# A two-layer hybrid decoder step on one core: sample state updates moved into the feed-forward stage, with four smaller changes of order

## The chip, the cores and the metric

The kernel runs on one core of one Trainium2 chip. The metric is the device time of one execution in microseconds (us); where several runs are given, the median is used, and the spread stands beside it.

## What is computed

The reference is one inference step of two layers. A layer normalises x, projects it, runs three mixers side by side on parts of the projection, multiplies their joined outputs with `w_out`, and adds; then a gated feed-forward network (FFN) with a causal convolution of width 3 follows. At the end there is one more norm. Cut to what matters here:

```python
h = rmsnorm(x);  proj = h @ w_in
rq, rk, rv, rg, su, gq, gk, gv, gg, glr = split(proj)
o_ret, s_ret_new = retention_chunked(rotary(rq), rotary(rk), rv, s_ret)   # 6 heads of 64
o_ret = groupnorm(o_ret) * silu(rg)
o_s5 = gelu(s5_scan(su));  o_s5 = o_s5 * sigmoid(o_s5 @ glu_w + glu_b)
o_gla, s_gla_new = gla_chunked(gq, gk, gv, log_sigmoid(glr @ gate_w + gate_b) / 16, s_gla)   # 4 heads
o_gla = rms(o_gla) * silu(gg)
x = x + concat([o_ret, o_s5, o_gla]) @ w_out
a, gate = split(rmsnorm(x) @ ffn_w_in)
x = x + (gelu(conv3(a)) * gate) @ ffn_w_out
y = rmsnorm(x)                                                            # after both layers
```

Two groups of tokens share the weights: a prompt of 512 tokens that starts from a zero state, and eight samples of 4 new tokens each (32 columns) that start from given states. Besides y, the new state of each mixer is an output. For a sample, the output of a head needs the old state; the new state (old state, decayed, plus keys times values) is needed by nothing else in the step. That is true of retention and of gated linear attention (GLA) alike.

## The kernel before

Activations lie with features on the 128 partitions and the 544 tokens as columns: `x` is eight tiles of 128x544. A product with a weight goes through `product()`: weights and activations are split into a high and a low part, and three passes over two halves of 272 columns make six matmuls of 128x272 for each 128 rows of the weight (a k-tile). A product with eight k-tiles has 48 such matmuls. `weights()` runs ahead of them: for each half unit (four k-tiles, 128x512) a DMA on SyncE's queue (`raw`, three in advance), a cast on ScalarE (`ws<-raw`, the high part), a subtraction on VectorE (`ws<-raw,ws`, the low part); four such `ws` tiles are held. In the trace the matmuls of weight products read `mm<-a,ws`; the small matmuls of the mixers write tiles called `m`. The accumulators `mm` have two buffers in PSUM, the small ones `m` have four. The SBUF pool `c` has ten buffers.

A layer has three stages. `in_proj` makes 24 tiles of 128 columns in the order of `IN_TILES`; `evac` takes each out of PSUM and, for most, multiplies it by `r`, the reciprocal norm that is computed beside the first product. Between these products the streams of the mixers run: GLA and retention in chunk pairs (0,1), (2,3) and the sample chunk (`gla_sample`, `ret_sample`), each followed by a norm (`gla_norm1`, `ret_norm1`) and a tail that transposes the result back; S5 in `s5_fetch` (tables) and `s5_stream` (u is written to DRAM as `ud` and read back as `w<-ud`, then scans and a gated output). `out_proj` makes eight tiles in two parts of four k-tiles; `MIX_TILES` says in which order the eight mixer tiles are used (0 to 2 retention, 3 and 4 S5, 5 to 7 GLA). `ffn` makes 22 pairs of up and gate tiles, with the down products in groups, and in layer 2 its last group is `end()`: the final norm is done for two column halves, `scaled()` prepares x and `output(h)` writes half h.

The order on every engine is made by a planner, `Order`. Each stream is a generator that yields between pieces; it has a priority (`PRI`), the main stream with the weight products has the last one. A piece is issued when its due time on TensorE's planned clock has come and, for priorities with a limit in `LIMITS`, when the engines are planned to be idle enough. `spawn(prio, gen)` starts a stream, `fire(name)` sets an event, `yield name` waits for one. A result is a fixed order of instructions on each engine; the waits between engines are semaphores. All instructions are issued in one helper, so that the trace gives L166 for all of them (L165 in the changed kernel), and they are told apart by their tiles.

At the end of `gla_sample`, after its outputs, stands the update of the sample's state:

```python
ks, vs = stacked(st["kt"], GH * 64, 2), stacked(m.gv[4], GH * GV, 1)   # ACT CAST d<-d, DVE d<-d,d
kt2 = pair_keys(ks, GH)                                                # ACT c<-d,const
vm = pair_values(vs, hd * GV, 2 * GV)                                  # ACT c<-d,const
pe.matmul(kv, lhsT=kt2[...], rhs=vm[...], start=True, stop=True)       # PE m<-c,c
add(ve, sv, sv, kv);  mul(ve, sv, sv, es[...])                         # DVE c<-c,m and c<-c,es
```

`ret_sample` ends in the same way, with a decay by a constant on ScalarE (`c<-c` 128x256) in the place of `c<-c,es`. Each then writes the state out by DMA. The states `S_` of these updates are the tiles that were loaded for the outputs, 2 of 384 KB for GLA and 3 of 256 KB for retention in each layer.

## Time and profile before

| | |
|---|---|
| median of 3 runs | 1382.23 us (1379.76 to 1383.33) |
| the profiled execution, its own time | 1385.73 us |
| its span, first to last instruction | 1383.9 us |
| mean granted TensorE clock | 0.981 of full speed |
| TensorE busy | 1341.8 us, 97% of the span |
| VectorE, ScalarE, GpSimd busy | 881.7, 603.4, 136.2 us |
| DMA | 133.64 MB, 97 GB/s |

The page is one execution, taken by the hardware profiler. A busy time of TensorE is not TensorE at its peak: the granted clock says at which of its two levels (1.2 and 2.4 GHz) it ran. In rows of a timeline, "[1.88 <-DVE c]" means that the engine was idle for 1.88 us before this group and that an instruction of VectorE on a tile c ended the wait; "x66" is the number of instructions in the group. PE is TensorE, PEld its weight loads, DVE VectorE, ACT ScalarE, POOL GpSimd, SP SyncE.

### The profile page before, as it was taken

How to read it: one execution, taken by the hardware profiler on the slowest of the kernel's cores; microseconds unless marked ns; L12 is line 12 of the kernel's file. 1: busy time of each engine (PE TensorE's matmuls, PEld its weight loads, DVE VectorE, ACT ScalarE, POOL GpSimd, SP SyncE). 2: the span in 40 equal slices, each digit the busy share in tenths (PEclk: the TensorE clock that was granted, in tenths of full speed). 3: DMA queues.
4: the chain of work that ended last, by engine and by line, in shares of the span. 5: the costliest groups of instructions: out<-in, count | busy, mean ns of one | idle time of the engine just before them, and what ended most of it. 6: DMA issues, size and time to landing. Idle time of an engine off the chain costs nothing.

```text
span 1383.9 us, 27885 instructions
## 1 busy us (share of the span) xinstructions
PE 1341.8 (97%) x11016; PEld 1314.1 (95%) x11016; DVE 881.7 (64%) x1773; ACT 603.4 (44%) x1256; POOL 136.2 (10%) x358
## 2 busy tenths in 40 slices
PE   6998998999999999999999999999999999999996
PEld 5997997999999999999998999999999999999996
DVE  7876787675567776555667475778655365455456
ACT  4556744553333443333444676346333233233232
POOL 0060000001100460100000000000111011011001
PEclk9999998899999999999998999999999999999998
DMA  5412332232223244323254322123222322322231
GB/s 184 132 51 71 105 98 86 70 94 88 92 80 104 93 131 127 131 67 109 73 169 141 102 80 93 54 91 117 84 84 77 100 92 74 96 92 81 89 98 65
DMA packets 88979, 133.64 MB, mean 97 GB/s; under 512 B 22352, under 2 KB 35088, under 8 KB 88848
## 3 DMA queue, kind: packets, MB, share of 16 engines
q1 hardware_dynamic: 88848, 131.86, 30.6%
q8 instruction: 87, 1.43, 0.4%
q14 instruction: 44, 0.36, 0.1%
HBM read 118.03 MB, written 12.61 MB: 94 GB/s over the span
## 4 chain that ended last, share of the span: by engine, by line
PE 90%; DVE 3%; ACT 2%; POOL 2%; DMA 1%; issue 1%; SPq 1%; DVEq 0%; ACTq 0%; POOLq 0%
PE mm L166 81%; PE m L166 9%; ACT c L166 1%; DVE c L166 1%; POOL a L166 1%; SPq L166 1%; DVE a L166 1%; ACT a L166 0%; DMA x<-in_x 0%; DMA w<-ud 0%; POOL c L166 0%; DVE ws L166 0%; POOL rtq L166 0%; POOL rot L166 0%; ACT ws L166 0%
## 5 line engine op out<-in xcount | busy, mean ns | idle before, releaser
L166 PE MATMUL mm<-a,ws 128*128 128x272 f32 x9408 | 1217.9, 290 | 13.2 <-ACT a L166 8.7
L166 PEld LDWEIGHTS mm<-a,ws 128*128 128x128 f32 x9408 | 1198.0, 190 | 20.1 <-ACT a L166 8.9
L166 ACT CAST ws<-raw 128x512 fp32r<-128x512 f32 (+2 forms) x424 | 249.2, 589 | 485.5 <-PE mm L166 369.2
L166 DVE TENSOR_TENSOR ws<-raw,ws 128x512 fp32r<-128x512 f32 (+2 forms) x424 | 274.5, 652 | 154.0 <-ACT ws L166 153.0
L166 DVE TENSOR_TENSOR c<-mm,r 128x544 f32<-128x544 f32 (+2 forms) x134 | 68.1, 535 | 132.9 <-PE mm L166 128.6
L166 DVE TENSOR_TENSOR x<-x,mm 128x544 f32<-128x544 f32 (+1 forms) x100 | 69.7, 697 | 40.3 <-PE mm L166 38.1
L166 DVE SCALAR_TENSOR_TENSOR w<-c,vec,w 128x560 f32<-128x560 f32 x88 | 71.5, 813 | 16.4 <-ACT w L166 14.6
L166 POOL COPY c<-c 128x2 f32<-128x2 f32 x88 | 34.5, 422 | 435.6 <-DVE c L166 435.6
L166 ACT CAST a<-c 128x544 fp32r<-128x544 f32 x44 | 28.6, 650 | 62.6 <-DVE c L166 52.9
L166 DVE TENSOR_TENSOR a<-c,a 128x544 fp32r<-128x544 f32 x44 | 32.2, 732 | 35.1 <-ACT a L166 35.1
L166 ACT COPY c<-mm 32x544 f32<-32x544 f32 (+1 forms) x60 | 36.4, 607 | 38.9 <-DVE a L166 27.1
L166 POOL MEMSET c<- 128x2 f32 (+4 forms) x54 | 8.6, 160 | 434.2 <-ACT c L166 106.1
L166 POOL TENSOR_TENSOR c<-c,w 128x32 f32<-128x32 f32 x44 | 25.9, 588 | 212.5 <-DVE c L166 175.2
L166 ACT ACTIVATE w<-c,vec 128x560 f32<-128x560 f32 x44 | 37.8, 860 | 8.5 <-DVE c L166 8.5
L166 DVE TENSOR_TENSOR c<-c,w 128x512 f32<-128x512 f32 x44 | 32.4, 737 | 0.0
L166 ACT ACTIVATE c<-c 128x256 f32<-128x256 f32 (+1 forms) x22 | 9.6, 463 | 49.6 <-DVE c L166 49.6
L166 ACT ACTIVATE a<-m,vec 128x128 f32<-128x128 f32 (+2 forms) x68 | 22.6, 413 | 19.1 <-PE m L166 18.9
L166 ACT ACTIVATE w<-w 128x560 f32<-128x560 f32 x44 | 29.6, 672 | 1.7 <-DVE w L166 1.7
L166 ACT ACTIVATE c<-x 128x544 f32<-128x544 f32 (+1 forms) x45 | 24.4, 567 | 7.1 <-DVE x L166 6.7
L166 DVE SCALAR_TENSOR_TENSOR a<-x,vec,a 128x544 fp32r<-128x544 f32 x32 | 24.8, 785 | 4.1 <-ACT a L166 3.3
L166 ACT ACTIVATE a<-x,vec 128x544 fp32r<-128x544 f32 x32 | 23.8, 753 | 7.1 <-DVE x L166 2.8
L166 ACT COPY c<-m 16x128 f32<-16x128 f32 (+3 forms) x51 | 16.6, 326 | 17.1 <-PE m L166 16.7
(187 smaller groups left out, 876.4 us busy)
## 6 DMA issues: line engine op xcount, KB each, us to landing
raw<-in_w_up SPq DMA_DIRECT2D x176, 256.0 KB, 2.8
raw<-in_w_in SPq DMA_DIRECT2D x96, 256.0 KB, 3.0
raw<-in_w_dn SPq DMA_DIRECT2D x64, 256.0 KB, 2.7
raw<-in_w_out SPq DMA_DIRECT2D x32, 256.0 KB, 3.0
raw<-in_w_dn SPq DMA_DIRECT2D x40, 128.0 KB, 2.3
x<-in_x SPq DMA_DIRECT2D x8, 272.0 KB, 5.9
out_y<-a SPq DMA_DIRECT2D x7, 272.0 KB, 2.2
c<-in_sgla SPq DMA_DIRECT2D x4, 384.0 KB, 5.1
```

The lines of the kernel that those rows point to most:

```text
L166: res = f(*args, **kw)
```

## The change

1. The updates of the sample states leave `gla_sample` and `ret_sample` and become streams of their own, `gla_update` and `ret_update`, with priority `late=6` (limit 0.0). They wait for the event `q{l}`, the norm between mixers and FFN, and load the states a second time: ten more DMAs in the two layers, 3 MB.
2. In layer 0, the first three products (su0, su1, gq0) are copied from PSUM to SBUF by ScalarE (`early`), before `r` is known; `evac` then reads the copy. Before, only su0 had a stream of its own, and it was read from PSUM.
3. `MIX_TILES` puts GLA's tiles first in `out_proj`, and S5's tile 4 into the second part.
4. The second table load of S5 (`kpxt`, in `s5_fetch`) waits for the event `U`, which is fired once the load of `w<-ud` is issued, in the place of `us`, which is fired when `ud` is written.
5. In `output`, half 0 is multiplied on VectorE, which takes `r` from PSUM and the gain in the same instruction (before: GpSimd, with a copy of `r`, after VectorE had scaled x by the gain). Of half 1's eight tiles three go to GpSimd (`POOL_OUT`), with a copy of `r` and a scaling of x by ScalarE; its output is written in six pieces, before five.

An unused filler of matmuls in the planner goes as well; it had no instruction in the program but one memset of its operand.

```diff
-MIX_TILES = [3, 4, 5, 6, 7, 0, 1, 2]
+MIX_TILES = [5, 6, 7, 3, 4, 0, 1, 2]
...
-OUT_KS = [[(0, 1), (2, 3), (4, 5), (6, 7)], [(0,), (1, 2), (3, 4), (5, 6), (7,)]]
+EARLY = 3
+
+OUT_KS = [[(0, 1), (2, 3), (4, 5), (6, 7)], [(0,), (5,), (1, 2), (6,), (3, 4), (7,)]]
+
+POOL_OUT = 3
...
-           rotor=3, rotor1=7, fetch=1, out=3)
+           rotor=3, rotor1=7, fetch=1, out=3, late=6)
...
-            r = SM([128, NT], "r", bufs=1) if self.h is None else None if self.h else M3([128, n])
+            r = SM([128, NT], "r", bufs=1) if self.h is None else None
...
-                yield f"us@{l}"
+                yield f"U@{l}"
...
         sy.dma_start(out=U, in_=m.ud.rearrange("s h g n -> (s h) g n"))
         yield
+        fire(m.n("U"))
...
         spawn(PRI["gt"], gla_tail(m, (4,), [st]))
+        spawn(PRI["late"], gla_update(m, st, es))
+
+    def gla_update(m, st, es):
+
+        l = m.l
+        yield f"q{l}"
+        S_ = [M3([128, 2, 4, GV]) for _ in range(2)]
+        for i in range(2):
+            sy.dma_start(out=S_[i].rearrange("p h q c -> p (h q c)"), in_=sgla_in[l, :, i * 8 * GV:(i + 1) * 8 * GV])
+        yield
         ks, vs = stacked(st["kt"], GH * 64, 2), stacked(m.gv[4], GH * GV, 1)
...
         spawn(PRI["rt"], ret_tail(m, (4,), [st]))
+        spawn(PRI["late"], ret_update(m, st))
+
+    def ret_update(m, st):
+        l = m.l
+        yield f"q{l}"
+        S_ = [M3([128, 2, 4, 64]) for _ in range(3)]
+        for i in range(3):
+            sy.dma_start(out=S_[i].rearrange("p h q c -> p (h q c)"), in_=sret_in[l, :, i * 512:(i + 1) * 512])
+        yield
         ks, vs = stacked(st["kt"][0:32].rearrange("p i c -> p (i c)"), RH * 64, 2), stacked(m.rv[4], RH * 64, 1)
...
-            if l == 0 and name == IN_TILES[0]:
-                spawn(0, evac(m, name, pre, i, ps))
+            if l == 0 and name in IN_TILES[:EARLY]:
+                spawn(0, early(m, name, pre, i, ps))
             else:
                 yield from evac(m, name, pre, i, ps)
+
+    def early(m, name, pre, i, ps):
+
+        t = M3([128, NT])
+        se.copy(t, ps)
+        yield
+        yield from evac(m, name, pre, i, t)
...
             yield from nrm[h].feed(x[j][:, cs])
-            if not h:
-                ts(ve, x[j][:, cs], x[j][:, cs], gf(j), None, ALU.mult)
+            if h and j >= 8 - POOL_OUT:
+                se.activation(out=x[j][:, cs], in_=x[j][:, cs], func=AF.Identity, scale=gf(j))
...
             r = rs_[f"r{L}.{h}"]
+            if h:
+                r_ = M3([128, HB])
+                se.copy(r_, r)
             for ks in OUT_KS[h]:
                 t = A([128, 4, HB])
                 for i, k in enumerate(ks):
-                    if not h:
-                        mul(po, t[:, i], x[k][:, cs], r)
+                    if h and k >= 8 - POOL_OUT:
+                        mul(po, t[:, i], x[k][:, cs], r_)
                     else:
                         stt(t[:, i], x[k][:, cs], gf(k), r, ALU.mult, ALU.mult)
+                if not h:
+                    yield 0
```

Because the planner makes the order, these edits move more than their own lines. Three places follow. A name's number is that of its allocation; `x6` at the end of a row is a run of equal rows.

The first place is TensorE at the end of layer 0's `in_proj` and the start of `out_proj`. `mm<-a,ws` are weight products, `m<-Sret`, `m<-d,c` and `m<-d,d` a retention chunk pair's output, `m<-a,c` S5's gate, `m<-c,c` state updates, `m<-a,a` the scores of the next chunk, `m<-const,...` transposes. Before, with the pieces between the shown ones left out:

```order
L166 MATMUL mm_2840<-a_148,ws_2740 128x272 x6
L166 MATMUL m_2911<-Sret,a_1243 128x128 x2
...
L166 MATMUL m_2911<-d_2019,c_2723 128x64 x6
L166 MATMUL m_2921<-d_2019,d_2738 64x64 x6
L166 MATMUL m_2941<-a_2699,c_2703 128x272
...
L166 MATMUL m_2952<-c_2712,c_2289 128x384
L166 MATMUL m_2956<-c_2712,c_2289 128x384
L166 MATMUL m_2963<-a_1243,a_1456 128x128
...
L166 MATMUL m_2983<-Sret,a_1243 128x128 x2
...
L166 MATMUL m_3010<-a_2699,c_2703 128x272
L166 MATMUL mm_2908<-a_2981,ws_2805 128x272 x6
L166 MATMUL m_3045<-a_1243,a_1456 32x32
```

After the change:

```order
L165 MATMUL m_2813<-const,a_1608 128x128 x2
L165 MATMUL mm_2781<-a_142,ws_2633 128x272 x6
L165 MATMUL m_2830<-a_2650,c_2654 128x272
...
L165 MATMUL m_2844<-Sret,a_1207 128x128 x2
L165 MATMUL m_2844<-Sret,a_1442 128x128
L165 MATMUL m_2844<-d_2031,c_2802 128x64 x6
L165 MATMUL m_2854<-d_2031,d_2817 64x64 x6
L165 MATMUL mm_2781<-a_143,ws_2670 128x272 x6
...
L165 MATMUL mm_2781<-a_146,ws_2670 128x272 x6
L165 MATMUL m_2900<-a_1207,a_1442 32x32
...
L165 MATMUL m_2914<-const,a_1608 32x128 x2
L165 MATMUL mm_2923<-a_139,ws_2724 128x272 x6
```

Before, 26 rows of mixer work stand in one block behind the last product of `in_proj`, and one k-tile of `out_proj` (`mm_2908<-a_2981`) stands between that block and the next. Now the same work begins earlier, in shorter pieces, with six to 24 matmuls of weight products between them; the state updates (`m<-c,c`) are gone from here.

The second place is VectorE in layer 0 at the norm of GLA's chunks 0 and 1 (`gv`). Here `c<-D,c` is a scan of S5 (a timeline calls it TENSOR_TENSOR_SCAN), `w<-w,w` a table of S5, `c<-c,a` both a rotary and a part of S5's scan. Before:

```order
L166 TENSOR_TENSOR ws_1257<-raw_1005,ws_1257 128x512
L166 SCALAR_TENSOR_TENSOR c_1297<-D_115_882,c_1203 128x256 x2
L166 TENSOR_TENSOR c_1245<-c_1245,a_720 128x544
L166 TENSOR_TENSOR w_1144<-w_1144,w_1235 128x1152
L166 TENSOR_TENSOR ws_1313<-raw_1086,ws_1313 128x512
L166 TENSOR_TENSOR c_1325<-c_1297,a_881 128x256
L166 TENSOR_TENSOR c_1326<-c_1297,a_881 128x256 x2
L166 TENSOR_TENSOR c_1325<-c_1297,a_881 128x256
L166 TENSOR_REDUCE gv_190_1334<-c_1160 128x4
L166 TENSOR_REDUCE gv_190_1334<-c_1291 128x4
```

After:

```order
L165 TENSOR_TENSOR s5so_595<-s5so_595,m_1282 128x32
L165 TENSOR_TENSOR c_1209<-c_1209,a_695 128x544
L165 TENSOR_TENSOR ws_1270<-raw_1060,ws_1270 128x512
L165 TENSOR_REDUCE gv_188_1316<-c_1146 128x4
L165 TENSOR_REDUCE gv_188_1316<-c_1267 128x4
L165 TENSOR_SCALAR gv_1319<-gv_188_1316 128x8
...
L165 SCALAR_TENSOR_TENSOR c_1437<-D_124_938,c_1280 128x256 x2
L165 TENSOR_TENSOR a_1207<-a_1207,c_1209 128x544
...
L165 TENSOR_TENSOR c_1471<-c_1437,a_937 128x256
L165 TENSOR_TENSOR c_1472<-c_1437,a_937 128x256 x2
...
L165 TENSOR_TENSOR w_1178<-w_1178,w_1247 128x1152
```

Before, the scan, the table sum, one more low part of a weight and four products `c<-c,a` stand ahead of the two reductions; now the reductions follow S5's small sums, one `c<-c,a` and one low part, and the rest comes behind the norm.

The third place is VectorE at the state updates of retention and GLA in layer 0. Before, inside `out_proj`'s first products (`x_89<-x_89,mm_2908` is the first sum of x, `rv` and `mu` belong to the retention norm of the sample chunk):

```order
L166 TENSOR_REDUCE mu_3136<-m_3104 128x6
L166 SCALAR_TENSOR_TENSOR c_3135<-mu_3136,m_3104 128x384
L166 TENSOR_TENSOR d_3140<-d_3063,d_3140 32x384
L166 TENSOR_TENSOR d_3144<-d_2021,d_3144 32x384
L166 TENSOR_TENSOR x_89<-x_89,mm_2908 128x544
L166 TENSOR_REDUCE rv_462_3176<-c_3135 128x6
```

After, in the FFN (`c<-mm,r` is the evacuation of an up product, `w<-c,vec,w` the convolution):

```order
L165 TENSOR_TENSOR c_3670<-mm_3673,r_3755 128x512
L165 TENSOR_TENSOR c_3670<-mm_3673,r_3755 128x8x4
L165 TENSOR_TENSOR ws_3767<-raw_3646,ws_3767 128x512
L165 TENSOR_TENSOR d_3807<-d_1760,d_3807 32x256
L165 TENSOR_TENSOR d_3811<-d_826,d_3811 32x384
L165 SCALAR_TENSOR_TENSOR w_3773<-c_3670,vec,w_3773 128x560 x2
...
L165 TENSOR_TENSOR ws_3984<-raw_3874,ws_3984 128x512
L165 TENSOR_TENSOR c_3790<-c_3790,m_3968 128x384
L165 TENSOR_TENSOR c_3790<-c_3790,es_256_1800 128x384
L165 TENSOR_TENSOR ws_4016<-raw_3916,ws_4016 128x512
```

The splits `d<-d,d` stood between the mean and the variance of the sample's retention norm, ahead of the first sum of x; now they stand between the first products of the FFN, with the updates `c<-c,m` and `c<-c,es` some products later.

## Rows read from the trace of the kernel before

**Rows 1.** The page, part 1: engine, busy time, share of span, instructions.
```profile
PE 1341.8 (97%) x11016; PEld 1314.1 (95%) x11016; DVE 881.7 (64%) x1773; ACT 603.4 (44%) x1256; POOL 136.2 (10%) x358
```

**Rows 2.** Windows: stretch, length, busy PE, PEld, DVE, ACT, POOL; clock, DMA share, GB/s.
```profile
218.00:262.00 44.00, 36.98 (x275) 31.77 (x274) 27.87 (x73) 18.39 (x45) 1.41 (x2) 0.81 0.18 55
300.00:345.00 45.00, 45.00 (x363) 45.00 (x362) 27.06 (x50) 17.64 (x30) 5.01 (x16) 1.00 0.26 83
715.00:740.00 25.00, 22.88 (x156) 20.47 (x156) 12.39 (x29) 7.87 (x13) 0.00 (x0) 0.80 0.59 186
```

**Rows 3.** Chain that ended last: start us, us, engine, tile, instructions.
```profile
307.68 171.09 PE mm L166 x1362
```

**Rows 4.** Timeline, PE, layer 0: start us, us, what [idle before <-releaser].
```profile
220.93 2.10 PE L166 MATMUL m<-a,c 128*128 128x272 f32 x8
...
232.00 3.39 PE L166 MATMUL m<-a,c 128*128 128x272 f32 x8
...
238.76 0.99 PE L166 MATMUL m<-const,c 128*128 128x128 f32 x6 [1.88 <-DVE c L166]
...
242.21 0.44 PE L166 MATMUL m<-c,c 128*32 128x64 f32 x8 [1.66 <-ACT c L166]
...
247.51 10.42 PE L166 MATMUL mm<-a,ws 128*128 128x272 f32 x66
```

**Rows 5.** Timeline of PE, layer 0, start.
```profile
33.06 8.52 PE L166 MATMUL mm<-a,ws 128*128 128x272 f32 x66 [0.90 <-DVE w L166]
...
107.33 1.08 PE L166 MATMUL m<-const,c 128*128 128x128 f32 x6 [1.78 <-DVE c L166]
110.91 6.68 PE L166 MATMUL mm<-a,ws 128*128 128x272 f32 x36 [2.51 <-ACT c L166]
```

**Rows 6.** Timeline of DVE, layer 0, 98 to 109 us.
```profile
98.85 1.27 DVE L166 TENSOR_TENSOR_SCAN c<-D,c 128x256 f32<-128x256 f32 x2
...
103.86 1.01 DVE L166 TENSOR_REDUCE gv<-c 128x4 f32<-128x384 f32 x2
```

**Rows 7.** Timeline of PE and DVE, layer 1.
```profile
728.27 1.24 PE L166 MATMUL m<-w,a 128*64 128x72 f32 x32 [2.12 <-DMA w<-ud]
...
923.82 4.80 PE L166 MATMUL mm<-a,ws 128*128 128x272 f32 x24
929.22 3.25 PE L166 MATMUL mm<-a,ws 128*128 128x272 f32 x24 [0.60 <-DVE x L166]
...
926.09 0.55 DVE L166 TENSOR_TENSOR d<-d,d 32x384 fp32r<-32x384 f32 x1 [0.99 <-ACT d L166]
```

**Rows 8.** Groups by line, ACT and DVE, whole span: busy, mean ns, idle before.
```profile
L166 ACT ACTIVATE c<-d,const 96x128 fp32r<-96x128 f32 (+3 forms) x48 | 17.3, 436 | 0.0
...
L166 ACT CAST d<-d 32x384 fp32r<-32x384 f32 (+1 forms) x16 | 7.7, 483 | 0.3
...
L166 DVE TENSOR_TENSOR c<-c,m 128x384 f32<-128x384 f32 (+1 forms) x14 | 8.5, 606 | 4.8 <-PE m L166 4.8
...
L166 DVE TENSOR_TENSOR c<-c,es 128x384 f32<-128x384 f32 x8 | 4.5, 558 | 0.3
...
L166 DVE TENSOR_TENSOR d<-d,d 32x384 fp32r<-32x384 f32 (+1 forms) x8 | 4.1, 516 | 9.5 <-ACT d L166 9.5
```

**Rows 9.** The same view of ACT, different shapes kept apart.
```profile
L166 ACT COPY c<-mm 128x544 f32<-128x544 f32 x12 | 7.3, 612 | 11.3 <-PE mm L166 11.3
...
L166 ACT ACTIVATE c<-c 128x256 f32<-128x256 f32 x12 | 4.3, 411 | 0.5 <-DVE c L166 0.5
```

**Rows 10.** Timeline of POOL and DVE, end, 1368 to 1381 us.
```profile
1368.76 6.18 POOL L166 TENSOR_TENSOR a<-x,c 128x272 f32<-128x272 f32 x8 [24.17 <-ACT c L166]
...
1370.66 0.42 DVE L166 TENSOR_TENSOR x<-x,mm 128x272 f32<-128x272 f32 x1
...
1372.93 0.60 DVE L166 TENSOR_TENSOR nt<-ny 128x3 f32<-128x3 f32 x1
...
1377.30 3.36 DVE L166 SCALAR_TENSOR_TENSOR a<-x,vec,m 128x272 f32<-128x272 f32 x8 [1.56 <-PE m L166]
```

More of the change, by code (lines that the diff above doesn't have):

```diff
@@ L59 @@
 MARGIN = 25.0
-WARM = 0
-FILLER = ("filler",)
-FILL, FILL_MARGIN = 230.0, 150.0
 V_NMG, V_NFG, V_RNG, V_RNB, V_D, V_GLUB, V_GB, V_GG = 0, 8, 16, 19, 22, 24, 26, 28
@@ L110, in __init__ @@
         self.events = {}
-        self.filler = None
         self.streams = []
@@ L137, in used @@
         self.uses[key] = self.uses.get(key, 0) + 1
-        if self.plan and key[0] != FILLER and self.uses[key] == self.plan["uses"].get(key):
+        if self.plan and self.uses[key] == self.plan["uses"].get(key):
             self.back(name)
@@ L229, in fire @@
         self.events[name] = self.mark
-    def fill(self, now):
-        then = self.free["pe"]
-        n = int((then - now - FILL_MARGIN) / FILL)
-        if n > 0 and len(self.pools.get("m", [0] * 4)) > 1:
-            self.sid = FILLER
-            self.free["pe"] = now
-            self.filler(n)
-            self.free["pe"] = max(then, self.free["pe"])
     def spawn(self, prio, gen):
@@ L257, in run @@
                 self.free["pe"] = min(max(whens[id(s)], now + busy - LIMITS[s[0]]) for s in can)
-                if self.filler and self.free["pe"] < INF:
-                    self.fill(now)
                 assert self.free["pe"] < INF, [(s[4], self.plan["takes"].get((s[4], self.step.get(s[4], 0)))) for s in can]
@@ L354, in trunk @@
     half = cp.tile([128, 1], F32, name="halfc")
-    warm = cp.tile([128, 1, 128], BF16, name="warm")
     trim = cp.tile([128, 2, 128], U8, name="trim")
@@ L1693, in trunk @@
     with tc.manual_schedule():
-        po.memset(warm, 1.0)
         sy.dma_start(out=vec, in_=vec_in)
@@ L1720, in masks @@
             yield
-        def filler(n):
-            ps = MX()
-            for _ in range(n):
-                pe.matmul(ps, lhsT=warm[:, 0], rhs=warm.to_broadcast([128, 4, 128]), start=True, stop=True)
-            order.back(ps.name)
-        order.filler = None
-        order.sid = FILLER
-        filler(WARM)
-        order.sid = ()
         order.free["pe"] = 0.0
```

## Prediction

> **What bounds the kernel now.** I read the page first: TensorE is busy for 1341.8 of 1383.9 us [rows 1]. Some 42 us of idle time are all that a better order can remove directly, and much of that is the start and the end. The chain of waits says the same: its longest piece is 171 us of nothing but weight matmuls, 1362 of them [rows 3]. That piece also gives the price of a matmul at full clock, 171.09 / 1362 = 0.1256 us, so a k-tile (six) costs 0.754 us and a product of eight k-tiles 6.03 us. Then I took windows. In the FFN TensorE is busy for the whole of 300 to 345 us at clock 1.00, while VectorE and ScalarE have 18 and 27 us free of 45 [rows 2]. In 218 to 262 us, where layer 0's mixers end and `out_proj` begins, it is busy for 36.98 of 44, at a mean clock of 0.81 [rows 2]. So there are two losses there: idle time, and slow matmuls behind it. The timeline shows the second: the same eight S5 gate matmuls took 2.10 us at 220.93 and 3.39 us at 232.00, and 66 weight matmuls at 247.51 took 10.42 us, where full speed is 66 × 0.1256 = 8.29 [rows 4]. Between these lie waits of 1.9 and 1.7 us for VectorE and ScalarE [rows 4]. A wait before a block of small matmuls thus costs its own length and about as much again in clock.
>
> **The mixers' end in layer 0** (parts 1 and 3 of the change). The window 218 to 262 has 44 − 36.98 = 7.0 us of idle time; 44 × (1 − 0.81) = 8.4 us is the clock's share [rows 2]. Together they are 15.4 us, and this is the upper end. The changed order spreads the block of mixer rows between weight products, so that a result which TensorE had to wait for comes due behind 0.75 to 3 us of other work; the state updates, with their splits and scalings, are out of the way. What may stay: the order has one place where a scores product follows a single k-tile, and the norm of the sample chunk is still a chain through VectorE. If two waits as large as the present two stay (1.88 + 1.66 [rows 4]) with as much again for the clock, the gain is 15.4 − 3.5 − 3.5, about 8.5. I take 13.5, near the upper end, because most of the waits shown end on work that now has a product ahead of it, and allow 2 us for short new ones.
>
> **GLA's first norm in layer 0.** TensorE waits 1.78 us for the normed result, then 2.51 us for copies, and the next 36 weight matmuls take 6.68 us where 36 × 0.1256 = 4.52 [rows 5]: 6.5 us in all is the upper end. On VectorE the reductions of this norm begin at 103.86; a scan of S5, and behind it table work, a low part and four products, were begun at 98.85 [rows 6]. In the new order these stand behind the norm, so it can end up to 5.0 us sooner; the second wait (a rotary that holds an accumulator) goes only in part, because the rotary stands behind the norm too. I take 3.0, the middle of 0.5 and 6.5. Against this, the changed order puts S5's table transposes right ahead of the 16 matmuls that read their two copies: two copies of 128x512 at nearly the 0.61 us of the nearest row [rows 9], less what the transposes themselves cover. I take −0.7, between 0 and −1.5.
>
> **Early copies.** At 33.06 TensorE waits 0.90 us for VectorE to empty the first accumulator, which it can only do once r is known [rows 5]. A copy by ScalarE at 0.61 us [rows 9] needs no r. I take the whole 0.9 (0 to 0.9): three products' copies are 1.8 us on ScalarE, beside 18 us of matmuls. The wait for the norm's sum ahead of it stays.
>
> **Layer 1.** Its `out_proj` has the same cause in small: 24 weight matmuls took 4.80 us (3.01 at full speed), then 0.60 us of waiting for x, which VectorE adds late because of two splits `d<-d,d` that wait 0.99 us for ScalarE [rows 7]. The splits go: 1.8 + 0.6 = 2.4 us, which I take (2.0 to 2.8). S5's load of u ends a wait of 2.12 us at 728.27 [rows 7]. Part 4 of the change moves a table load behind it, but the load of u already stands ahead of it in SP's queue, so only one table load and one weight load change places. I take 0 (0 to 0.3).
>
> **The end.** Half 0's eight products on GpSimd took 6.18 us, 0.77 each, beside the chain of half 1's norm [rows 10]. Some of VectorE's steps ran slow meanwhile: a step on three columns took 0.60 us at 1372.93, the others of its kind 0.16. Without GpSimd there that chain is about 1.5 us shorter; six of half 0's products (0.42 us each [rows 10]) now stand on VectorE in the middle of it and give 1.0 back. The last eight steps, 3.36 us [rows 10], become five, about 2.1, with three on GpSimd (2.3) beside them, less a scalar copy and one more DMA in the queue. I take a gain of 1.0 (up to 1.5). Whether the two engines run side by side decides the lower end. The row shows that a VectorE step which takes one operand from PSUM was not slowed beside GpSimd: x<-x,mm took 0.42 us at 1370.66 [rows 10], and the new products take r from PSUM too. One after the other, they would need 3 × 0.77 + 5 × 0.42 = 4.4 instead of 3.36, and with the other terms the end gives −1.3. The Trainium skill, Perfetto Trace Analysis, section Optimizing Scalar/DVE Operations, warns that GpSimd and VectorE share an SBUF read port, so that moving work between those two might not help; by that rule the end is −1.3 and the sum 2.3 smaller. The trace agrees for the small steps (0.60 against 0.16) and not for the one with a PSUM operand.
>
> **What is put into the FFN.** Per layer, ScalarE gets (17.3 + 7.7 + 4.3) / 2 = 14.7 us and VectorE (8.5 + 4.5 + 4.1) / 2 = 8.6 us [rows 8, 9]. In the order they lie over some five products, 30 us, in which each engine has 12 to 18 us free by the window of the FFN [rows 2]: ScalarE about 18, VectorE 12. It fits, with ScalarE near 90% there. I cost it at nothing; the cover is the four `ws` tiles that run ahead. The state loads are 1.5 MB per layer beside 83 GB/s at a DMA share of 0.26 [rows 2], also nothing, though they stand in front of weight loads in SP's queue.
>
> **The sum.** 0.9 + 3.0 − 0.7 + 13.5 + 2.4 + 0 + 1.0 + 0 = 20.1 us. The profiled execution took 1385.73 us (span 1383.9 and 1.8 around it), 3.5 above the median of 1382.23. A gain of 20.1 from the median gives **1362 us**. The lower ends add up to 0 + 0.5 − 1.5 + 8.5 + 2.0 − 1.3 = 8.2, that is 1374; the upper ends to 0.9 + 6.5 + 15.4 + 2.8 + 0.3 + 1.5 = 27.4, that is 1355.
>
> **Rivals.**
> - *Half of it.* The pieces that are spread out wait anyway: one k-tile of 0.75 us is shorter than a chain through two engines, and each wait pulls the clock down again. Then layer 0 gives about 5 instead of 13.5 and GLA's norm 1 to 2, in all 10, so 1372. For it: even now weight matmuls stand between waits, and still ran slow [rows 4]. Against: the new order gives most results more than one k-tile. Chance 0.20.
> - *Slower, by the FFN.* There TensorE is never idle, so there is no slack: every us by which a weight's low part or an accumulator comes late is lost. Both engines' moved work is 2 × (14.7 + 8.6) = 46.6 us. If all of it came out, the time would be 1382.2 + 46.6 − 20.1 = 1408.7. It turns the sign once 20.1 / 46.6 = 43% of it is exposed. Against it: the FFN's idle engines [rows 2]. Chance 0.05.
> - *The load of u comes early as well.* The window 715 to 740 loses 25 − 22.88 = 2.1 us idle and 25 × 0.20 = 5.0 us of clock [rows 2]. If the later table load frees the DMA engines, all 7.1 go: 1355. The order says that u's load already leaves first. Chance 0.06.
> - *Nothing to speak of.* The waits move to other places, and the state loads hold up weight loads: 1378 to 1386. Chance 0.07.
> - *One port at the end*, as worked out above: 1364. It is inside my forecast and has 0.3 of it; the rest does not depend on it.
>
> **The numbers.** A run can tell about 0.3%, 4 us, from no change. My forecast, 1355 to 1368, has 0.62; with half of it (0.20) and u's load (0.06), faster has 0.88. Same has 0.07, slower 0.05. The range of 1355 to 1374 holds the forecast and most of the second case; outside are the slow cases and the tails.
>
> **What would show it.** In the profile after: 218 to 262 us with a clock above 0.95 and under 2 us of idle time; no 2.5 us wait behind GLA's first norm; no wait ahead of the second batch of weight matmuls in the first 35 us; `d<-d,d` and `c<-c,m` inside the FFN with TensorE still busy throughout; the wait for `w<-ud` at about 2 us as now. I am wrong if the FFN shows waits of TensorE for `ws` or for an accumulator, if layer 0's clock still falls below 0.9 in that stage, or if the end is longer than before.

## The result and the profile after

The change makes the kernel faster by 1.2%: 1367.52 us, the median of 4 runs (1364.20 to 1373.29), against 1382.78 (4 runs, 1379.76 to 1387.76) beside it. The ratio is 0.9882 with a 95% interval of 0.9855 to 0.9909. The forecast was 1362 us in a range of 1355 to 1374, with most of its weight on 1355 to 1368; the time lies at the upper end of that. The profiled execution has a span of 1365.6 us, 18.3 less than the one before, at a mean clock of 0.988.

TensorE's busy time of the changed kernel, from part 1 of the page (before: [rows 1]), fell with the clock loss; the work is the same:

```profile
PE 1331.7 (98%) x11016; PEld 1307.0 (96%) x11016; DVE 879.8 (64%) x1770; ACT 603.5 (44%) x1262; POOL 131.7 (10%) x352
```

Three windows of the changed kernel, with the columns of [rows 2]. Layer 0's stage has no idle time left, but a clock of only 0.92. In the FFN, ScalarE went from 17.64 to 27.42 us of 45 and VectorE from 27.06 to 32.87, and TensorE lost 0.32 us there. Layer 1's stretch behind the load of u runs at clock 1.00:

```profile
218.00:262.00 44.00, 44.00 (x369) 42.01 (x368) 32.53 (x76) 16.48 (x37) 0.10 (x1) 0.92 0.25 81
300.00:345.00 45.00, 44.68 (x354) 44.41 (x353) 32.87 (x53) 27.42 (x59) 5.55 (x16) 1.00 0.37 121
715.00:735.00 20.00, 18.63 (x205) 17.06 (x205) 17.28 (x42) 9.92 (x15) 0.12 (x1) 1.00 0.46 161
```

To see where the time went I compared the two traces at points that both pass: VectorE adds each output and down product to x, 100 times in the same order. The changed kernel is ahead by this much at some of them:

| point | ahead of before, us |
|---|---|
| end of `out_proj`, layer 0 | 12.95 |
| first down product, layer 0 | 10.93 |
| end of layer 0 | 10.66 |
| first sum of `out_proj`, layer 1 | 17.91 |
| end of `out_proj`, layer 1 | 20.04 |
| from the first down product of layer 1 on | 18.01 |
| end of the span | 18.3 |

The two steps back by 2.0 us in the FFNs are the state updates: their matmuls left the mixers and cost TensorE 1.7 us in each FFN, and there they wait once for ScalarE, 0.3 us. So layer 0 up to its first down product is worth 10.9 us net, the rest of its FFN loses 0.3, layer 1 up to its output product gives 7.2, that product 2.1 less the 2.0 of layer 1's own step back, and the end 0.3.

TensorE in layer 0 after the change (timeline as in [rows 4, 5]). The first wait at GLA's norm went from 1.78 to 0.38 us, the second grew from 2.51 to 3.23, and two waits for S5's tables stand at 143 and 145 us. Late in the sample chunk's small matmuls, which start at 237.16 and have no wait among them, and behind them the clock falls: the eight `m<-c,c` at 240.92 took 0.44 us, where such a group took 0.32 just before, and the 48 weight matmuls that follow take 8.77 us, where full clock is 6.03:

```profile
105.50 0.99 PE L165 MATMUL m<-const,c 128*128 128x128 f32 x6 [0.38 <-DVE c L165]
109.72 7.06 PE L165 MATMUL mm<-a,ws 128*128 128x272 f32 x42 [3.23 <-ACT c L165]
...
143.38 0.31 PE L165 MATMUL m<-w,a 128*64 128x72 f32 x2 [0.61 <-DMA a<-c]
145.55 0.25 PE L165 MATMUL m<-w,a 128*64 128x72 f32 x1 [1.87 <-DMA a<-c]
...
167.80 1.27 PE L165 MATMUL m<-w,a 128*64 128x72 f32 x32 [0.24 <-ACT a L165]
...
237.16 0.43 PE L165 MATMUL m<-d,c 32*128 32x64 f32 x2
...
240.92 0.44 PE L165 MATMUL m<-c,c 128*32 128x64 f32 x8
241.29 8.77 PE L165 MATMUL mm<-a,ws 128*128 128x272 f32 x48
```

TensorE in layer 1 (compare [rows 7]). The wait for u fell from 2.12 to 1.37 us, and the 12 weight matmuls behind it from 3.09 to 1.77. The 48 behind layer 1's sample chunk still take 7.63 us, where full clock is 6.03. First the kernel before, a line of its timeline and the two windows of 10 us behind its wait for u (clock 0.57 and 0.92):

```profile
731.46 3.09 PE L166 MATMUL mm<-a,ws 128*128 128x272 f32 x12
...
728.27:738.27 10.00, 9.99 (x59) 7.78 (x60) 4.83 (x14) 3.63 (x6) 0.00 (x0) 0.57 0.38 148
738.27:748.27 10.00, 10.00 (x99) 9.85 (x99) 8.80 (x19) 4.46 (x7) 0.12 (x1) 0.92 0.18 55
```

Then the changed kernel:

```profile
716.86 1.27 PE L165 MATMUL m<-w,a 128*64 128x72 f32 x32 [1.37 <-DMA w<-ud]
...
719.17 1.77 PE L165 MATMUL mm<-a,ws 128*128 128x272 f32 x12
...
906.03 7.63 PE L165 MATMUL mm<-a,ws 128*128 128x272 f32 x48
```

The end, TensorE, VectorE and GpSimd (compare [rows 10]). The three-column steps take 0.16 us again. The six products of half 0 at 1350.24 are ahead of the last sum, and TensorE's wait for that sum is 1.94 us, 1.00 before. Five products on VectorE (2.13) and three on GpSimd (2.19) run side by side:

```profile
1353.73 1.64 PE L165 MATMUL m<-ones,c 128*128 128x1 f32 x12 [1.94 <-DVE c L165]
1357.20 1.46 PE L165 MATMUL m<-const,ny 128*128 128x128 f32 x6 [1.83 <-DVE ny L165]
...
1350.24 2.54 DVE L165 SCALAR_TENSOR_TENSOR a<-x,vec,m 128x272 f32<-128x272 f32 x6
...
1355.81 0.16 DVE L165 TENSOR_TENSOR nt<-ny 128x3 f32<-128x3 f32 x1
...
1359.12 2.13 DVE L165 SCALAR_TENSOR_TENSOR a<-x,vec,m 128x272 f32<-128x272 f32 x5 [1.98 <-ACT c L165]
...
1359.17 2.19 POOL L165 TENSOR_TENSOR a<-x,c 128x272 f32<-128x272 f32 x3 [32.59 <-ACT c L165]
```

### The profile page after: what moved, and what is told of

It is laid out like the page before. It is cut to its first block, busy times and chain, and to the rows that moved or that the text cites. A ratio compares the mean times of both kernels' runs of the same rounds, so it can differ in the third digit from the quotient of the medians.

```text
span 1365.6 us, 27885 instructions
## 1 busy us (share of the span) xinstructions
PE 1331.7 (98%) x11016; PEld 1307.0 (96%) x11016; DVE 879.8 (64%) x1770; ACT 603.5 (44%) x1262; POOL 131.7 (10%) x352
## 4 chain that ended last, share of the span: by engine, by line
PE 89%; issue 3%; DVE 2%; POOL 2%; ACT 2%; DMA 1%; SPq 0%; POOLq 0%; ACTq 0%; DVEq 0%
PE mm L165 81%; PE m L165 8%; ACT c L165 1%; DVE c L165 1%; POOL a L165 1%; DMA x<-in_x 0%; DMA w<-ud 0%; POOL c L165 0%; ACT a L165 0%; SPq L165 0%; DVE ws L165 0%; POOL rot L165 0%; DVE a L165 0%; POOL rtq L165 0%; DMA c<-in_sgla 0%
## 5 line engine op out<-in xcount | busy, mean ns | idle before, releaser
L165 DVE TENSOR_TENSOR c<-mm,r 128x512 f32<-128x512 f32 (+2 forms) x133 | 67.3, 534 | 115.6 <-PE mm L165 111.2
```

Source lines behind the costliest of these rows:

```text
L165: res = f(*args, **kw)
```

## The experiments

All times are medians; each ratio is to runs of the kernel before on the same chip, whose medians were 1384 to 1387. The first four rows were run on one chip, the next two with "sample block spread" and "copies ahead of the rotary product" on a second, the others on a third; across chips it is the ratios that compare. Diffs are against the changed kernel unless said otherwise.

| kernel | us (runs) | ratio, 95% interval |
|---|---|---|
| changed, again | 1368.19 (6) | 0.9879 [0.9859, 0.9900] |
| table load as before | 1372.90 (6) | 0.9909 [0.9884, 0.9934] |
| updates inline | 1390.24 (7) | 1.0042 [1.0026, 1.0058] |
| old tile order | 1373.61 (6) | 0.9927 [0.9906, 0.9948] |
| before, only updates moved | 1376.23 (6) | 0.9929 [0.9902, 0.9956] |
| updates inline, old tile order | 1401.94 (6) | 1.0106 [1.0075, 1.0138] |
| no early copies | 1372.17 (6) | 0.9905 [0.9876, 0.9934] |
| old output | 1366.55 (6) | 0.9867 [0.9839, 0.9896] |
| sample block spread | 1373.40 (6) | 0.9914 [0.9885, 0.9943] |
| copies ahead of the rotary product | 1363.81 (6) | 0.9841 [0.9813, 0.9869] |
| the same, and products behind the last norm | 1361.96 (5) | 0.9831 [0.9803, 0.9860] |
| the same, without early copies | 1367.74 (6) | 0.9873 [0.9839, 0.9906] |

**The changed kernel again.** No edit.

> The changed kernel once more. Theory: its runs differ by whether the wait for u in layer 1 pulls the clock down; with a wait under 1.5 us the 20 us behind it run at clock 1.00 and the time is 1362 to 1368, with a wait of 2 us or more they run at about 0.75 and it is 5 to 6 us longer. Rival: the spread has nothing to do with that place, and the trace shows the stretch behind that wait at clock 1.00 at any length of the run.

1368.19 us, from 1363.73 to 1370.10, with mean clocks of 0.986 to 0.993 in the runs. The rival was nearer: the longest of the six runs is the one that was traced, and there u's wait was 1.60 us and the clock behind it 1.00. Where this execution lost 2.4 us against the other profile of the same kernel is layer 0, at S5's table waits near 145 us. There the waits are nearly the same as before (0.88 and 1.86 us against 0.61 and 1.87), yet this time the clock fell to 0.68, where it stayed at 1.00. Its window of 144 to 152 us, with the columns of [rows 2]:

```profile
144.00:152.00 8.00, 6.66 (x65) 5.47 (x66) 1.33 (x2) 1.91 (x6) 0.00 (x0) 0.68 0.82 263
```

The timeline of TensorE in the same trace:

```profile
143.17 0.31 PE L165 MATMUL m<-w,a 128*64 128x72 f32 x2 [0.88 <-ACT c L165]
145.34 0.25 PE L165 MATMUL m<-w,a 128*64 128x72 f32 x1 [1.86 <-DMA a<-c]
```

So the same wait sometimes costs clock and sometimes not. That is a likely part of the spread of a kernel's runs, whose mean clocks differ with their times. Differences of 2 to 3 us between two traces are not to be read without looking at the clock.

**The table load as before** (part 4 undone).

```diff
-                yield f"U@{l}"
+                yield f"us@{l}"
```

> Only the table load of layer 1 goes back ahead of one weight load, right behind the load of u. Theory: the two loads then share the DMA engines, u lands in about 5.9 us as before the change, TensorE waits about 2.1 us for it and loses some 5 us of clock behind it: 1372 to 1374, 5 to 6 us over the changed kernel. Rival: u came early for another reason (its write, or the traffic before it), the wait stays near 1.4 us and the time near 1367.5.

1372.90 us, 4.7 over the changed kernel beside it; but the six runs reach from 1364.18 to 1375.65 and the intervals of the two ratios overlap, so the times alone leave it open, and the place itself has to show it. Both traces issue the load of u at 711.60 us, but with a table load right behind it, it ends TensorE's wait at 718.09, not 716.86. The wait is 2.62 us and the 12 weight matmuls behind it take 3.09 us again; at layer 1's first output sum this kernel is 2.7 us behind. Its timeline of TensorE:

```profile
718.09 1.27 PE L165 MATMUL m<-w,a 128*64 128x72 f32 x32 [2.62 <-DMA w<-ud]
...
720.42 3.09 PE L165 MATMUL mm<-a,ws 128*128 128x272 f32 x12
```

The other traces agree. With the table load directly behind it, the load of u took 5.95, 6.08 and 6.45 us from issue to landing (three traces); with a weight load of half the size directly behind and the table load one place later, 4.68 to 5.68 us in ten traces and 6.28 in one. That is the theory in kind: the order of two lines in SP's queue decides how soon u lands; that the loads share the DMA engines is the likely reason. The size is 2.7 us at the place, not the 5 to 6 expected; a further 1.5 us came behind the sample chunk, where 48 weight matmuls took 8.94 us instead of 7.63 in this execution, and is no part of it.

**The updates inline** (part 1 undone) and **the old order of tiles** (part 3 undone).

```diff
-        spawn(PRI["late"], gla_update(m, st, es))
+        yield from gla_update(m, st, es, S_)
...
-        spawn(PRI["late"], ret_update(m, st))
+        yield from ret_update(m, st, S_)
```

(the updates then start at once and use the states already loaded)

> The state updates go back into the mixers, all other parts stay. Theory: their absence is the larger part of what layer 0 gained, and layer 1's output product loses 2 us again: 1374 to 1378, with waits for VectorE and ScalarE and a clock under 0.9 around layer 0's first output products. Rival: the gain of layer 0 came from the other edits that move the order, and this costs 0 to 3 us: 1367 to 1370.

```diff
-MIX_TILES = [5, 6, 7, 3, 4, 0, 1, 2]
+MIX_TILES = [3, 4, 5, 6, 7, 0, 1, 2]
```

> Only the order of the mixers' tiles in the output product goes back. Theory: with the updates gone, either order finds its tiles ready in time, and the time stays within 2 us of the changed kernel, 1366 to 1370. Rival: GLA first is what lets retention's end run beside weight products in layer 0, and without it 4 to 8 us come back: 1371 to 1376.

Inline, the updates cost 22 us: 1390.24, more than either theory gave and slower than the kernel before. At the end of layer 0's `out_proj` this kernel is 22.2 us behind the changed one. The windows of 218 to 262 and 262 to 310 us lose 7.4 and 3.4 us of idle time, with clocks of 0.84 and 0.96; one wait is for an activation of S5's output on ScalarE, one for the sum into x. The two windows of the kernel with the updates inline:

```profile
218.00:262.00 44.00, 36.60 (x291) 31.48 (x290) 28.48 (x75) 19.09 (x45) 1.47 (x2) 0.84 0.20 60
262.00:310.00 48.00, 44.64 (x368) 42.77 (x368) 36.68 (x65) 28.80 (x59) 0.45 (x2) 0.96 0.35 111
```

The timeline of TensorE in the same trace:

```profile
231.43 3.99 PE L165 MATMUL m<-a,c 128*128 128x272 f32 x8 [3.41 <-ACT a L165]
...
273.86 4.77 PE L165 MATMUL mm<-a,ws 128*128 128x272 f32 x24 [2.12 <-DVE x L165]
```

The old order of tiles costs 5.4 us (1373.61), near the rival's middle. Layer 0 is 8.5 us behind the first profile of the changed kernel. Of these, 3.1 arise near 145 us, where the two kernels still have the same order on TensorE: that is the loss at S5's tables that the changed kernel's second profile shows too. Another 3.7 are one wait that neither theory named, for the load of retention's states in the sample chunk, in its timeline:

```profile
239.43 0.32 PE L165 MATMUL m<-c,c 128*32 128x64 f32 x8 [3.72 <-DMA c<-in_sret]
```

**Only the updates moved, on the kernel before**, and **both undone**.

```diff
 (against the kernel before)
+        spawn(PRI["late"], gla_update(m, st, es))
+    def gla_update(m, st, es):
+        l = m.l
+        yield f"q{l}"
...
+        spawn(PRI["late"], ret_update(m, st))
```

> The kernel before with nothing but the state updates moved into the FFN. Theory: this alone is the larger part of the whole gain, since the updates inline cost 22 us when everything else was changed: 1370 to 1375, layer 0's output product 8 to 12 us earlier, layer 1's wait for u still above 2 us. Rival: the gain needs the new order of the tiles too, and alone the updates give 2 to 5 us: 1379 to 1382.

> The changed kernel with both the updates back in the mixers and the old order of the tiles. Theory: what made the updates so dear in the mixers was GLA first, whose tiles then wait behind the updates; with the old order most of these 22 us are gone and the time is near the kernel before, less the later table load and the early copies: 1378 to 1384. Rival: early copies and the other edits spoil layer 0's order by themselves, and it stays above 1387.

The updates alone give 9.7 us (1376.23 against 1385.89 beside it): the larger part, as the theory had it, though the time lies 1.2 us above its range. Layer 0's trace is then 11.1 us ahead at the end of `out_proj`, of the changed kernel's 12.95. In layer 1 its wait for u is 2.74 us. With both undone, the time is 1401.94: not the 1378 to 1384 of the theory, and the rival was right. In layer 0 this kernel differs from the one before by the early copies alone, and is 15.8 us behind it at the end of `out_proj`. The planner's order with the copies and with the updates inline has one wait of 5.5 us there for a norm's result from VectorE, and a clock of 0.77 in 218 to 262 us. So the parts are not a sum. Moving the updates is worth 9.7 us alone, 22 with the other parts and GLA first, 25 (by the ratios) to 28 (by the medians) with the other parts and the old order. GLA first is worth 5 us with the updates moved, 9 to 12 with them inline.

**No early copies** (part 2 undone) and **the old output** (part 5 undone).

```diff
-            if l == 0 and name in IN_TILES[:EARLY]:
-                spawn(0, early(m, name, pre, i, ps))
+            if l == 0 and name == IN_TILES[0]:
+                spawn(0, evac(m, name, pre, i, ps))
```

> Only the three early copies are undone (su0 alone keeps its own stream, read from the accumulator). Theory: they gave 0.9 us at the start, and the order that they bring behind it gave little in layer 0 (the kernel with only the updates moved had layer 0's output product within 2 us of the changed kernel): 1367 to 1370. Rival: the order that they bring is needed, or harmful: more than 2 us away on either side, with the waits of layer 0 between 95 and 262 us in other places.

```diff
-                        stt(t[:, i], x[k][:, cs], gf(k), r, ALU.mult, ALU.mult)
+                        mul(po, t[:, i], x[k][:, cs], r)
```

(and the rest of part 5, as in the diff of the change)

> Only the final output goes back to GpSimd for half 0. Theory: by the two traces, from the last weight matmul to the end of the span it was 14.1 us before and 13.8 after, so this costs 0.3 us, up to 1: 1367.5 to 1369, and the three-column steps of the last norm run slow again. Rival: the new output is worth what was forecast, 1.0 us or more.

Without the copies the wait of 0.91 us at 33.5 us is back, and layer 0's `out_proj` ends 0.6 us ahead of one profile of the changed kernel and 3.0 ahead of the other. The median is 1372.17, but its six runs lie from 1368.07 to 1376.46 and the intervals of the ratios overlap, so its sign stays open. What the trace does show is that the order at GLA's first norm belongs to the copies: without them its two waits are 1.74 and 2.50 us, as in the kernel before (1.78 and 2.51), where the changed kernel has 0.38 and 3.23; and for S5's tables TensorE waits 1.16 us near 135 us and 2.00 near 196, where the changed kernel has its two waits near 145.

With the old output the time is 1366.55, not different from the changed kernel's. From the last weight matmul to the end its trace has 13.98 us; the two of the changed kernel have 13.81 and 13.77. But other traces with the changed output have 13.8 to 14.6 us there, so what part 5 is worth can't be told from nothing.

**The sample block spread.**

```diff
-        pair_out(ops_, Q, S_, heads, 64, 0)
-        yield 1
-        pair_out(ops_, Q, S_, heads, 64, 1)
+        for part in range(6):
+            pair_out(ops_, Q, S_, heads, 64, part, 6)
+            yield 1500
```

(`pair_out` takes the number of parts as one more argument)

> In the changed kernel the 60 small matmuls of retention's sample output are split by head, with one or two k-tiles of weight products between. Theory: it is this block, not a wait, behind which the clock falls in layer 0 (near 240 us) and in layer 1 (near 906 us); spread out, both stretches run at clock 1.00 and 3 to 5 us go: 1363 to 1365. Rival: the small matmuls slow the clock wherever they stand, or the norm behind them comes later: 1367 to 1370.

1373.40 us, 5 longer by the ratios too, whose intervals just overlap: not the theory's time, and beyond the rival's. The clock did what the theory said: 1.00 in layer 0's stage, where both profiles of the changed kernel have 0.92, and in layer 1 the 60 weight matmuls behind the block took 7.80 us, near full clock. But the block now ends later, its norm too, and retention's tiles are late for the second part of `out_proj`. In layer 1 TensorE waits 0.56 and 1.10 us for them and the clock falls there (0.91 in 915 to 935 us). The window of layer 0's stage in the spread kernel:

```profile
218.00:262.00 44.00, 44.00 (x383) 41.31 (x382) 30.74 (x74) 17.64 (x41) 0.84 (x2) 1.00 0.27 87
```

The timeline of TensorE in the same trace:

```profile
926.60 0.51 PE L165 MATMUL mm<-a,ws 128*128 128x272 f32 x2 [0.56 <-ACT a L165]
928.22 28.66 PE L165 MATMUL mm<-a,ws 128*128 128x272 f32 x214 [1.10 <-DVE a L165]
```

Against the first profile of the changed kernel, layer 0 gains 1.0 us at this place and layer 1 loses 3.0 at its own; the rest of the 6 us by which this trace is longer is clock at S5's tables and behind u's wait, ahead of the block and no part of it. In layer 1 more came back as waits than the clock gave, so spreading it in this way is no gain. That the block is the cause is likely and not shown. In the ten traces of kernels with the updates moved and the block in one piece there are 18 places where 48 weight matmuls follow it: in 6 they took 6.30 us (three of them in the kernels with the table load and the output as before), in 12 they took 7.43 to 8.94. (With the updates inline it was 8.65 to 10.17 in all four.) Two places at full clock in the spread kernel could be chance at that rate.

**Copies ahead of the rotary product.** `evac` of a retention query or key has one VectorE product and four ScalarE copies that read the same accumulator. In the order of the program, the first copy waits for the product: ScalarE was idle for 11.06 us ahead of it at GLA's norm, where the product stands behind that norm on VectorE (timeline of the changed kernel):

```profile
107.22 2.45 ACT L165 COPY c<-mm 32x544 f32<-32x544 f32 x4 [11.06 <-DVE a L165]
```

```diff
-            mul(ve, m.qkraw[a // 2][:, a % 2], ps, m.rcs[:, 0])
             sw = M3([128, NT])
             for z in range(4):
                 se.copy(sw[z * 32:z * 32 + 32], ps[(z ^ 1) * 32:(z ^ 1) * 32 + 32])
+            mul(ve, m.qkraw[a // 2][:, a % 2], ps, m.rcs[:, 0])
```

> In the changed kernel ScalarE's four copies out of a rotary accumulator stand ahead of VectorE's product from it, nothing else. Theory: the two engines read the same accumulator one after the other in program order, so at GLA's first norm ScalarE waits idle behind VectorE's norm; ahead of it, the 3.2 us wait of TensorE near 107 us falls to about 1.8, the clock behind it falls less, and 1.5 to 3 us go: 1364 to 1366. Rival: elsewhere VectorE then waits for ScalarE, and the time stays within 1 us of 1367.5 or is 1 to 3 us longer.

1363.81 us, 3.7 to 4.4 us under the changed kernel and more than the theory had; the intervals of the ratios overlap by 0.001, so the gain is likely, not beyond doubt. TensorE's 3.23 us wait became 0.76 (the other 1.52), and 42 weight matmuls take 5.54 us, 7.06 before; full clock is 5.28. The timeline of TensorE and ScalarE with the reads exchanged, where the copies start when the product ends, at 99.41 instead of 107.22 us, and only VectorE's read is left to wait for:

```profile
106.86 0.93 PE L165 MATMUL m<-const,c 128*128 128x128 f32 x6 [1.52 <-DVE c L165]
108.54 5.54 PE L165 MATMUL mm<-a,ws 128*128 128x272 f32 x42 [0.76 <-DVE a L165]
...
99.41 2.46 ACT L165 COPY c<-mm 32x544 f32<-32x544 f32 x4 [3.03 <-PE mm L165]
```

Layer 0 ends 8.1 us ahead of the changed kernel's trace. Of these, 2.5 are the place behind the sample block, which ran at full clock in this execution (6.30 us against 8.77). 4.9 are lost again in layer 1, part of it clock behind u's wait (1.59 us, clock 0.83 in the next 10). But 2.9 us of it are the rival's: three waits of TensorE for VectorE (0.66, 0.57 and 1.71 us) that the changed kernel does not have, because VectorE now stands behind ScalarE's copies at layer 1's GLA norms. TensorE and VectorE there, with the reads exchanged:

```profile
814.78 0.52 PE L165 MATMUL m<-const,c 128*128 128x128 f32 x3 [1.71 <-DVE c L165]
...
811.08 0.72 DVE L165 TENSOR_TENSOR a<-mm,a 128x544 f32<-128x544 f32 x1 [5.58 <-ACT c L165]
```

The same exchange helps where VectorE is the late one and hurts where ScalarE is. Which of the two should read first was not tried place by place.

**The same, and six products of half 0 behind the last norm**; and **without the early copies**.

```diff
             y = rsqrt_small(self.ps[:, 0:len(cols)], D, len(cols), "n")
+            if self.h:
+                fire(f"y{L}")
...
-                if not h:
-                    yield 0
                 sy.dma_start(out=y_out[:, ks[0]:ks[-1] + 1, cs], in_=t[:, 0:len(ks)])
+                if not h and ks[0] == 0:
+                    yield f"y{L}"
+                    yield (1,)
```

> The changed kernel with the copies ahead of VectorE's rotary product and, at the end, six of half 0's products moved behind the last norm's chain on VectorE. Theory: both gains add up, 4 us of the first and about 1.1 of the second (1.7 by which the last sum of x comes sooner, less 0.6 for what does not fit into VectorE's idle time before the last eight products): 1361.5 to 1364; from the last weight matmul to the end 12.5 to 13 us. Rival: what moves is on the path there too, and the end stays at 13.8 us: 1363.5 to 1365.

> The same without the early copies. Theory: the copies cost little and give 0.4 us at the start, so it is 0 to 2 us slower than with them. Rival: the order that the copies bring is the worse one in layer 0, and it is 2 to 5 us faster without them.

1361.96 us (1360.89 to 1364.58) is the best of all, 6.2 under the changed kernel's 1368.19; both intervals touch at 0.986, so the order of the two is likely, not beyond doubt. From the swapped copies alone (1363.81) the times don't tell it apart. From the last weight matmul to the end it has 13.04 us, 0.7 to 0.8 less than the changed kernel and less than any trace with the end as it was. In its timeline VectorE's last eleven products run without a gap:

```profile
1349.93 0.43 DVE L165 TENSOR_TENSOR x<-x,mm 128x272 f32<-128x272 f32 x1
...
1353.40 4.57 DVE L165 SCALAR_TENSOR_TENSOR a<-x,vec,m 128x272 f32<-128x272 f32 x11
```

Without the early copies it is 1367.74, 5.8 longer, more than either theory gave; its profiled execution is one of the shorter ones (span 1360.9 us), and its runs reach from 1362.32 to 1375.81. The cause of that spread stays open. The copies' other pair (1372.17 against 1368.19) has the same sign, so that they probably help; no trace shows where.

## Why the prediction was right, and where its steps were not

**The mixers' end in layer 0 (13.5 us forecast).** The upper end was 15.4, of which 7.0 was idle and 8.4 clock. The idle time went whole; of the clock 44 × (1 − 0.92) = 3.5 us stayed. The step that failed is the one that put the clock's loss behind the waits: behind the block of 60 small matmuls, which has no wait in it, the clock fell as well, as it does in 12 of 18 such places. A line of [rows 7] shows this already: no wait stands right ahead of the 24 weight matmuls at 923.82 us that took 4.80. That leaves about 11.9 of 13.5. (The updates' matmuls are no part of it: they were work, not loss.)

**GLA's first norm (3.0) and the transposes (−0.7).** The norm did come sooner: its reductions began at 101.95 us, not 103.86, 1.9 sooner where 5.0 was the most. But the copies behind it waited for VectorE's rotary product, so that the second wait grew; idle time went from 4.29 to 3.61 us and the loss of clock behind it from 2.16 to 7.06 − 5.28 = 1.78, in all 1.1. The swapped copies show what the step missed: the second wait belonged to the order of two readers of one accumulator. The transposes cost 0.24. Not in the forecast were two waits at 143 to 146 us for S5's tables, 2.5 us where one of 1.39 stood before, and 0.6 at 131.84 us. By the run without the copies, all of this order came with part 2.

**Early copies (0.9).** The wait is gone, but some products later the trace is only 0.37 us ahead: the 42 weight matmuls ahead of that place, behind the wait for the norm's sum, took 7.83 us, 6.86 before. That is clock; the other traces of the experiments have 6.99 to 7.81 there.

**Together** layer 0 was forecast at 16.7 and gave 10.9 up to its first down product.

**Layer 1's load of u (0).** This was the rival with 0.06, and it came: 0.75 us of wait, and the 10 us behind it at clock 1.00 instead of 0.57 with the next 10 at 0.92, 5.1 us, in all 5.9 of the rival's 7.1. The step that failed is "only one table load and one weight load change places": what stands directly *behind* a load in the queue delays it, by about 1.2 us here. Not all of the 5.9 is the table load's, though: undone, it cost 2.7 us at this place, and how far the clock falls behind a wait of 2 us or more differs between traces (last section). The rest of layer 1's 7.2 us is GLA's update, which left with its matmuls and a wait.

**Layer 1's output product (2.4).** The waits went (0.6 and 0.3, 0.9 in all), but the clock's loss of 1.8 did not (7.63 − 6.03 = 1.6 now): it is the place behind the small matmuls again. The 0.9 is the place's own; all of the layer's moved matmuls, GLA's too, are paid for by the 2.0 in the FFN, and with them counted here 0.1 is left.

**The end (1.0).** It gave 0.3. The norm's chain is 1.5 us shorter as forecast (a wait of 3.30 became 1.83) and the last products took 2.1; but the last sum came 0.9 later, the first product waits 0.4 for ScalarE's copy from the same accumulator, and the output's DMAs end 4.2 us after the last product, 3.2 before. VectorE's products with an operand in PSUM were not slowed beside GpSimd, 0.43 us each. So the rival by which the two engines would run one after the other did not come. The three-column steps took 0.16 us without GpSimd; beside it the first two took 0.16 to 0.17 too and the next three 0.60 to 0.68, again so in the kernel with the old output. The Trainium skill, Perfetto Trace Analysis, section Optimizing Scalar/DVE Operations, says that the two share an SBUF read port, so that moving work between them might not help; the trace agrees for those three steps, and not for the products that read r from PSUM.

**The FFN (0).** Right: ScalarE's 9.8 and VectorE's 5.8 us more in 300 to 345 us cost TensorE 0.32 us of idle time, in a wait of the updates' own matmuls. With it the updates cost 2.0 per layer there. Where the rest of layer 0's FFN lost another 0.3 stays open.

That the sum came out near was in good part luck, because two errors met: layer 0 was 5.8 us too high, its FFN 0.3, layer 1's output product and the end 3.0, and layer 1 up to its output product was 7.2 too low. 20.1 were forecast; the two traces differ by 18.3 and the medians by 15.3.

## What to carry to other kernels

Work that no later step needs, like a state's update, belongs beside a stage where TensorE is the only full engine; in the stage where the other engines are late it costs more than its own time, in waits and in the clock that often falls behind them. With an order made by a planner, parts of a change don't add: run each part alone and each undone. Before a wait is put down to an engine's load, look at which reader of a shared accumulator stands first, and which load stands directly behind the awaited one in a shared queue; then try it place by place.

## What the runs showed that was not expected

TensorE's clock fell behind work without a wait: after a block of 60 matmuls of 64 columns, the 48 weight matmuls at 241.29 us took 8.77 us, where full clock is 6.03. It did so in 12 of 18 places, and with the same order of TensorE's instructions in one execution and not in another: 8.77 and 8.78 us in the changed kernel's two traces, 6.30 in those with the old table load and the old output.

Behind a wait for u the clock depends on the wait, but not on it alone. These are the waits in all fourteen traces and the clock in the 10 us behind them: 1.26 us, 1.00; 1.36, 1.00; 1.36, 0.83; 1.37, 1.00; 1.52, 1.00; 1.59, 0.83; 1.60, 1.00; 1.68, 1.00; 1.90, 0.66; 2.12, 0.57; 2.45, 1.00; 2.62, 0.83; 2.74, 0.66; 3.19, 0.50. Of the eight shorter ones six left the clock at 1.00, of the six longer ones one. What else decides is open.
